# An extra ScalarE copy of a mixed RWKV projection from PSUM to SBUF, one multiply on VectorE, and smaller weight pools in the GLA stage

## The chip, the cores and the metric

The kernel runs on one core of one Trainium2 chip. The metric is the time of one execution on the device in microseconds (us), lower is better. The engines of the core work side by side and each takes its own instructions strictly in the order of its queue: TensorE (PE; its weight loads are listed apart as PEld), VectorE (DVE), ScalarE (ACT), GpSimd (POOL) and SyncE (SP, which here only issues transfers). They wait for each other through semaphores. PSUM is the memory into which TensorE writes its sums; a PSUM bank holds 512 float32 numbers in each of 128 partitions. SBUF is the working memory.

## What is computed

One layer of a decoder: a normalised input `h` (2048 tokens, 1024 channels) is projected once, and the projection feeds three causal mixers (RWKV-7, MLA attention, chunked gated linear attention or GLA), whose gated results are merged and projected again.

```python
h = rms_norm(x, norm_pre); proj = h @ w_in
(c_q, c_kv, k_rope, u_rwkv, g_q, g_k, g_v, g_lat, br_gate, merge_gate) = split(proj)
# RWKV: every channel is mixed with the token before, then split
u_prev = pad(u[:, :-1], one zero row in front)
u = u + (u_prev - u) * mu            # = u * (1 - mu) + u_prev * mu
r, k, v, lw, la = split(u)           # 512, 512, 512, 64, 64 channels
... recurrence over the tokens, head by head ...
y = (y - mean) * rsqrt(var + RWKV_GN_EPS) * ln_w + ln_b + bonus
# merge
ys = stack([y_mla, y_rwkv, y_gla]) * silu(br_gate)
merged = sum(sigmoid(merge_gate) * (ys @ w_branch_out)); x + rms_norm(merged @ w_out)
```

## The kernel before

The program is one stream for each engine, written out by a scheduler: the source is run once, every instruction gets a priority (`tc.high_priority(...)`), and a list scheduler with a modelled timeline sets the order on each engine. So an edit at one place can move instructions at many others. Tiles come from pools with a fixed number of buffers; an instruction that writes a new tile waits until the last reader of the buffer's old tile is done.

The stages follow each other: RWKV (`phase_rwkv`), a short stage for latents, MLA, GLA (`phase_gla`), merge. Matmuls are made in three passes for accuracy: `mm3` (L133 to L135) multiplies the high part of the weights with the high and the low part of `h`, and the low part of the weights with the high part of `h`. Weights therefore go through `load_w` (L121): a transfer issued by SyncE brings `w_raw`, ScalarE rounds it to `w_hi` (L118), and GpSimd subtracts to get `w_lo` (L119). One projection unit takes a block of 512 tokens and 128 output channels: `load_w8` makes four weight parts of 2 x 128 channels each, and each part feeds six matmuls of 128x512, 24 for a unit, all into one PSUM bank. Two banks (`psd0`, `psd1`, both called `psd` in the profile) are used in turn, in the RWKV stage and again in the GLA stage.

In the RWKV stage TensorE is filled with such units. Those of the RWKV input itself go through `mixed` (L387): there are 13 for each of the four blocks of tokens, 52 in all. One of the 13 has a single output tile `lwla` of 512 tokens; the other twelve write `r`, `k` or `v` in two halves of 256 tokens (`outs`, u = 0 and 1), which are separate tiles. `mixed` empties the bank so: for each half ScalarE multiplies by 1 - mu (L395), then VectorE adds mu times the sums shifted by one token (L397). Then VectorE adds the token carried over from the block before (L400) and copies the bank's last column to `carry` (L402). In the built order the ScalarE multiply of the second half waits for the VectorE instruction of the first half: the two engines take turns at the bank. The next unit of this bank starts when L402 is done.

Beside the units run the serial parts of RWKV: `within`, `inverses`, `whole`, `prepare` and `chain` work on 16 groups of 256 tokens and two head pairs. `chain` (L522) ends a group with a normalisation over each head: VectorE computes the inverse root (`k.rsqrt`), GpSimd multiplies `ysb` by it (L590), TensorE turns the result (L594) and VectorE writes `yo` (L600). `plain` and `gates` units fill up TensorE; their banks are emptied by a ScalarE copy (L317).

In the GLA stage the class `Gates` (L884) supplies the filling: 36 gate projections for the first three token blocks. `until` (L910) loads the weights of a gate once (L917, four parts with 4 raw and 5 rounded buffers) and uses them either for one block or for the two blocks 1 and 2 one after the other. There are 108 units of 24 matmuls, 32 of the loads serve two blocks. A ScalarE copy empties each bank (L926) and a transfer writes the result out (L927).

Of the kernel before, what the change touches and what calls it, by code (L numbers as in the profile page):

```python
# [9 lines left out]
F32 = mybir.dt.float32  # L10
# [3 lines left out]
ALU = mybir.AluOpType  # L14
# [10 lines left out]
TB = 512  # L25
# [45 lines left out]
class Ctx:  # L71
# [19 lines left out]
    def pool(self, name, bufs, **kw):  # L91

        if kw.get("space") != DRAM:
            kw["reuse_waits"] = "tile"
        return self.tc.tile_pool(name=name, bufs=bufs, **kw)
# [233 lines left out]
def phase_rwkv(k, pl, x, pos, w_rwkv, w_up2, w_more, w_gate, y_dram, more, pre, rope_dram):  # L329
# [3 lines left out]
    tc, nc = k.tc, k.nc  # L333
    with ExitStack() as st:
# [3 lines left out]
        t1 = pool("rw_t1")  # L338
# [12 lines left out]
        carry = per.tile([128, 13], F32, name="carry")  # L351
# [35 lines left out]
        def mixed(h, n, outs):  # L387


            ps = pl.sums()  # L390
            k.project(ps, pl.weights(w_rwkv[n]), h, slice(0, TB))
            mu = k.p("mu", n)
            m = TB // len(outs)
            for u, o in enumerate(outs):
                nc.scalar.mul(o, ps[:, u * m:u * m + m], imu[:, n:n + 1])  # L395
                i = u == 0
                nc.vector.scalar_tensor_tensor(out=o[:, int(i):m], in0=ps[:, u * m - 1 + i:u * m + m - 1], scalar=mu,  # L397
                                               in1=o[:, int(i):m], op0=ALU.mult, op1=ALU.add)
            o = outs[0]
            nc.vector.scalar_tensor_tensor(out=o[:, 0:1], in0=carry[:, n:n + 1], scalar=mu, in1=o[:, 0:1],  # L400
                                           op0=ALU.mult, op1=ALU.add)
            nc.vector.tensor_copy(carry[:, n:n + 1], ps[:, TB - 1:TB])  # L402

        idx = lambda q, hd, j: q * 4 + j * 2 + hd

# [115 lines left out]

        def chain(G, mr, T, bkt, rv, at):  # L522

            B, g, u, ar, bv, uv = (G[n] for n in ("B", "g", "u", "ar", "bv", "uv"))
            Z = state[g]
            by_head = lambda a: a.rearrange("p (q h v) -> p q h v", q=2, h=2)

# [9 lines left out]
            for cc in range(4):  # L537
                j, e_ = cc // 2, cc % 2
                asl, rsl = halves(e_)
                for q in range(2):  # L540
                    for hd, hs in heads:
                        m = nc.tensor.matmul(pA[:, q, hd], lhsT=ar[hs, q, cc, :], rhs=Z[hs, q, :], start=True, stop=True)
# [5 lines left out]
                for q in range(2):  # L548
                    for hd, osl in enumerate((asl, rsl)):
                        hc = slice((2 * q + hd) * 64, (2 * q + hd) * 64 + 64)  # L550
                        m = nc.tensor.matmul(pU[osl, q * 64:q * 64 + 64], lhsT=T[asl, idx(q, hd, j), :], rhs=rhs[asl, hc],
                                             start=True, stop=True)
# [5 lines left out]
                for q in range(2):  # L558
                    for hd, hs in heads:
                        hc = slice((2 * q + hd) * 64, (2 * q + hd) * 64 + 64)  # L560
                        m = nc.tensor.matmul(pZ[hs, q, :], lhsT=bkt[:, q, cc, hs], rhs=uv[:, j, e_, hc],
                                             start=True, stop=True)
# [18 lines left out]
            y4 = ysb.rearrange("p j (h v) -> p (j h) v", v=64)  # L581
# [5 lines left out]
                nc.scalar.activation(out=ysq, in_=y4[:, 4 * j:4 * j + 4], func=AF.Square)  # L587
                nc.vector.tensor_reduce(out=va[:, 4 * j:4 * j + 4], in_=ysq, axis=AX.X, op=ALU.add)
            rs = k.rsqrt(t2, va, 1.0 / 64, GN_EPS, "gn", bufs=1)
            nc.gpsimd.tensor_tensor(out=y4, in0=y4, in1=rs.unsqueeze(2).broadcast_to([128, 8, 64]), op=ALU.mult)  # L590
            po = ps_q.tile([128, 2, 256], F32, name="psq")
            for q in range(2):
                for j in range(2):
                    m = nc.tensor.transpose(po[:, q, j * 128:(j + 1) * 128], ysb[:, j, q * 128:(q + 1) * 128], k.ident)  # L594
                    if q == j == 0:
                        at(m, 14)
            for q in range(2):
# [3 lines left out]
                                               in1=bv[:, q, :], op0=ALU.mult, op1=ALU.add)  # L601
# [122 lines left out]
        n = 4 * NB  # L724
        blk, G, W, P, R = {}, {}, {}, {}, {}
# [10 lines left out]
        def project_group(i):  # L736
# [3 lines left out]
            if g == 0:  # L740
                lwla = t1.tile([128, TB], F32, name="lwla", bufs=1)
                mixed(blk["h"], 0, [lwla])
                nc.scalar.activation(out=lwla[0:64], in_=lwla[0:64], func=AF.Tanh)
                blk["l"] = lwla
            h, lwla = blk["h"], blk["l"]
            t = {m: [t1.tile([128, 2, 256], F32, name=m, bufs=RB) for _ in range(2)] for m in "rkv"}
            for q in range(2):
                for m in range(3):
                    mixed(h, 1 + 3 * (2 * g + q) + m, [o[:, q, :] for o in t["rkv"[m]]])
# [134 lines left out]
class Gates:  # L884
# [25 lines left out]
    def until(self, share, ps):  # L910

        k, nc = self.k, self.k.nc
        while self.todo and self.done < share * self.units:
            n, blocks = self.todo.pop(0)
            if n == 8 and blocks == (0,) or n == 0 and blocks == (1,):
                self.turned(blocks[0] + 1, ps)
            w = k.load_w8(self.wp, self.w_gate[n], 128, "w", parts=4, rb=4, hb=5)  # L917
            for B in blocks:
                i = self.turn % 2
                self.turn += 1  # L920
                p = self.ps[i].tile([128, TB], F32, name=f"psd{i}")
                k.filling = self.products
                k.project(p, w, self.h[B], slice(0, TB))
                k.filling = None
                o = self.op.tile([128, TB], F32, name="plain", bufs=2)
                nc.scalar.copy(o, p)  # L926
                nc.sync.dma_start(out=self.pre[n][:, B * TB:B * TB + TB], in_=o)  # L927
                self.done += 1
# [634 lines left out]
```

## Time and profile before

| what | value |
|---|---|
| time, three runs | 2982.84 us median (2981.33 to 2990.15) |
| the profiled execution, its own time | 2985.36 us |
| its span in the trace, first instruction to last | 2983.6 us |
| mean granted TensorE clock | 0.982 |
| busy: VectorE, ScalarE, GpSimd | 1718.7 us (58%), 1493.3 us (50%), 1444.3 us (48%) |
| TensorE in the chain that ended last | 65% of the span |

The profile lists busy time for each engine, groups of instructions by source line, and for a group the idle time of its engine just before it with the instruction that ended the wait ("idle before"; the arrow `<-` names who was waited for). Line numbers are those of the kernel before. A matmul row's duration is longer than the distance between two matmuls, since they are pipelined. The granted clock (PEclk) is the share of its full clock that TensorE was given.

### The profile page before, as it was taken

What the parts mean: (1) busy time and instruction counts of PE and PEld (TensorE: products, weight loads), DVE (VectorE), ACT (ScalarE), POOL (GpSimd) and SP (SyncE); (2) the same over time, 40 slices, a digit from 0 to 9 for tenths busy, and PEclk for the clock granted to TensorE, in tenths of its full rate; (3) what the DMA queues carried; (4) which work ended last, traced back from release to release, by engine and by line L of the source; (5) the groups of instructions that cost most, each with busy time, mean ns of one, the idle gap of its engine ahead of it and who ended that gap; (6) DMA issues with size and microseconds to landing.
All of it is one profiled execution on the core that took longest, in us unless ns stands there. A gap on an engine that the chain in (4) does not pass through costs nothing.

```text
span 2983.6 us, 54189 instructions
## 1 busy us (share of the span) xinstructions
PE 2861.1 (96%) x18496; PEld 2309.9 (77%) x18496; DVE 1718.7 (58%) x4642; ACT 1493.3 (50%) x3495; POOL 1444.3 (48%) x1865
## 2 busy tenths in 40 slices
PE   8998999999999999899999999999999999999998
PEld 6676767667777777689999887788788887777887
DVE  4647566666646524488888886544423313875444
ACT  5444444435444436587777775554433334554211
POOL 4543544444445445455454546775444424575322
PEclk9999999999999999899999999999999999999999
DMA  4333333223333434200000024444233226865422
GB/s 134 99 100 103 102 90 111 84 80 91 91 116 84 131 115 142 66 22 18 19 19 16 17 80 141 161 142 130 89 100 102 85 94 221 280 213 192 136 98 78
DMA packets 285173, 312.76 MB, mean 105 GB/s; under 512 B 77904, under 2 KB 234592, under 8 KB 284896
## 3 DMA queue, kind: packets, MB, share of 16 engines
q1 hardware_dynamic: 259088, 278.76, 30.1%
q10 hardware_dynamic: 25808, 30.54, 3.1%
q8 instruction: 146, 2.39, 0.3%
q14 instruction: 131, 1.07, 0.1%
HBM read 233.16 MB, written 76.02 MB: 104 GB/s over the span
## 4 chain that ended last, share of the span: by engine, by line
PE 65%; DVE 9%; DMA 3%; ACT 2%; issue 2%; POOL 1%; SPq 0%; ACTq 0%; DVEq 0%; POOLq 0%
PE psd L133 10%; PE psd L135 10%; PE psd L134 10%; PE pso L1307 4%; PE pst L1285 4%; PE pss L133 3%; PE pss L135 3%; PE pss L134 3%; PE psb L135 2%; PE psg L133 2%; PE psg L135 2%; PE psg L134 2%; PE psb L133 2%; PE psb L134 2%; PE psc L1070 1%
## 5 line engine op out<-in xcount | busy, mean ns | idle before, releaser
L119 POOL TENSOR_TENSOR w_lo<-w_raw,w_hi 128x256 fp32r<-128x256 f32 x848 | 649.9, 774 | 810.8 <-ACT w_hi L118 746.5
L133 PE MATMUL psd<-hh,w_hi 128*128 128x512 f32 x1952 | 798.7, 410 | 16.9 <-DVE carry L402 6.6
L135 PE MATMUL psd<-hh,w_lo 128*128 128x512 f32 x1952 | 787.5, 405 | 9.1 <-POOL w_lo L119 8.7
L134 PE MATMUL psd<-hl,w_hi 128*128 128x512 f32 x1952 | 780.6, 400 | 0.0
L118 ACT CAST w_hi<-w_raw 128x256 fp32r<-128x256 f32 x848 | 337.1, 404 | 532.3 <-PE psd L134 284.0
L133 PEld LDWEIGHTS psd<-hh,w_hi 128*128 128x128 f32 x1952 | 372.4, 191 | 109.1 <-ACT w_hi L118 17.1
L135 PEld LDWEIGHTS psd<-hh,w_lo 128*128 128x128 f32 x1952 | 372.5, 191 | 100.4 <-POOL w_lo L119 18.6
L134 PEld LDWEIGHTS psd<-hl,w_hi 128*128 128x128 f32 x1952 | 372.4, 191 | 75.5 <-issue 3.0
L1270 POOL TENSOR_SCALAR P<-P,nm 128x1024 f32<-128x1024 f32 (+2 forms) x192 | 165.5, 872 | 193.9 <-DVE nm L1267 157.6
L1290 DVE TENSOR_TENSOR tl<-pst,th 128x512 fp32r<-128x512 f32 (+2 forms) x352 | 193.9, 562 | 31.4 <-ACT th L1289 29.8
L1289 ACT CAST th<-pst 128x512 fp32r<-128x512 f32 (+2 forms) x352 | 165.2, 488 | 79.1 <-PE pst L1285 40.5
L1262 ACT ACTIVATE P<-P,nm 128x1024 f32<-128x1024 f32 (+2 forms) x192 | 172.3, 901 | 17.2 <-DVE nm L1258 13.8
L1248 DVE TENSOR_SCALAR_CACHE_REDUCE P<-pss 128x512 f32<-128x512 f32 (+3 forms) x288 | 168.5, 594 | 11.8 <-PE pss L135 8.7
L1285 PE MATMUL pst<-cs,P 128*128 128x128 f32 x1088 | 165.5, 274 | 0.2 <-DVE tl L1290 0.2
L1307 PE MATMUL pso<-th,v 128*128 128x256 f32 x576 | 150.1, 283 | 2.6 <-DVE yo L1315 2.6
L1307 PE MATMUL pso<-tl,v 128*64 128x256 f32 x576 | 139.1, 281 | 0.7 <-DVE tl L1290 0.7
L133 PE MATMUL pss<-kh,qh 128*128 128x512 f32 (+2 forms) x320 | 129.3, 404 | 5.1 <-issue 4.7
L1285 PEld LDWEIGHTS pst<-cs,P 128*128 128x128 f32 x1088 | 125.0, 140 | 8.9 <-DVE tl L1290 0.8
L119 POOL TENSOR_TENSOR wb_lo<-wb_raw,wb_hi 128x256 fp32r<-128x256 f32 x96 | 87.1, 913 | 83.7 <-ACT wb_hi L118 68.6
L1307 PEld LDWEIGHTS pso<-th,v 128*128 128x128 f32 x576 | 108.4, 188 | 12.1 <-DVE yo L1315 2.8
L135 PE MATMUL pss<-kh,ql 128*128 128x512 f32 (+2 forms) x320 | 117.0, 367 | 0.1
L134 PE MATMUL pss<-kl,qh 128*128 128x512 f32 (+2 forms) x320 | 117.0, 366 | 0.0
(391 smaller groups left out, 5640.5 us busy)
## 6 DMA issues: line engine op xcount, KB each, us to landing
w_raw<-in_w_gate_dram SPq DMA_DIRECT2D x448, 128.0 KB, 2.2
pre<-plain SPq DMA_DIRECT2D x144, 256.0 KB, 2.4
w_raw<-in_w_rwkv_dram SPq DMA_DIRECT2D x208, 128.0 KB, 2.2
w_raw<-in_w_more_dram SPq DMA_DIRECT2D x192, 128.0 KB, 2.2
h_g<-pre SPq DMA_DIRECT2D x48, 512.0 KB, 4.9
h_x<-in_x_dram SPq DMA_DIRECT2D x44, 512.0 KB, 4.3
more<-plain SPq DMA_DIRECT2D x48, 256.0 KB, 2.7
wb_raw<-in_w_br_dram ACTq DMA_DIRECT2D x96, 128.0 KB, 3.6
```

What stands on the lines that cost most here:

```text
L118: nc.scalar.copy(hi, src)
L119: (sub or nc.gpsimd).tensor_tensor(out=lo, in0=src, in1=hi.bitcast(F32), op=ALU.subtract)
L133: mm(out, lhsT=lhs[0], rhs=rhs[0], start=start, stop=False)
L134: mm(out, lhsT=lhs[0], rhs=rhs[1], start=False, stop=False)
L135: m = mm(out, lhsT=lhs[1], rhs=rhs[0], start=False, stop=stop)
L1248: nc.vector.tensor_scalar(out=pt[:, c0:c0 + f], in0=s_[:, 0:f], scalar1=-MLA_SCALE, scalar2=3e38, op0=ALU.mult, op1=ALU.min, accum_out=mx[ ...
L1262: nc.scalar.activation(out=pt[:, cw], in_=pt[:, cw], func=AF.Exp, bias=nm[:, 0:1], scale=-1.0, accum_out=nm[:, 1 + n:2 + n])
L1270: nc.gpsimd.tensor_scalar(out=pt[:, cw], in0=pt[:, cw], scalar1=nm[:, 1:2], scalar2=1.0, op0=ALU.mult, op1=ALU.mult)
L1285: nc.tensor.transpose(tp[:, kl, qt, :], P[qt][:, kt * 128:(kt + 1) * 128], k.ident)
L1289: nc.scalar.copy(flat(th)[:, r], flat(tp)[:, r])
L1290: nc.vector.tensor_tensor(out=flat(tl)[:, r], in0=flat(tp)[:, r], in1=flat(th)[:, r].bitcast(F32), op=ALU.subtract)
L1307: nc.tensor.matmul(d_, lhsT=l_, rhs=r_, start=kt == 0 and j == 0, stop=last and kl == 1 and j == 1)
```

## The change

```diff
@@ mixed @@
             for u, o in enumerate(outs):
                 nc.scalar.mul(o, ps[:, u * m:u * m + m], imu[:, n:n + 1])
+
+            now = t1.tile([128, TB], F32, name="now", bufs=2)
+            nc.scalar.copy(now, ps)
+            for u, o in enumerate(outs):
                 i = u == 0
-                nc.vector.scalar_tensor_tensor(out=o[:, int(i):m], in0=ps[:, u * m - 1 + i:u * m + m - 1], scalar=mu,
+                nc.vector.scalar_tensor_tensor(out=o[:, int(i):m], in0=now[:, u * m - 1 + i:u * m + m - 1], scalar=mu,
                                                in1=o[:, int(i):m], op0=ALU.mult, op1=ALU.add)
...
-            nc.vector.tensor_copy(carry[:, n:n + 1], ps[:, TB - 1:TB])
+            nc.vector.tensor_copy(carry[:, n:n + 1], now[:, TB - 1:TB])
@@ chain @@
+            i_ = 4 * B + 2 * g + u
...
-            nc.gpsimd.tensor_tensor(out=y4, in0=y4, in1=rs.unsqueeze(2).broadcast_to([128, 8, 64]), op=ALU.mult)
+            (nc.vector if i_ == n - 1 else nc.gpsimd).tensor_tensor(
+                out=y4, in0=y4, in1=rs.unsqueeze(2).broadcast_to([128, 8, 64]), op=ALU.mult)
@@ Gates.until @@
-            w = k.load_w8(self.wp, self.w_gate[n], 128, "w", parts=4, rb=4, hb=5)
+            w = k.load_w8(self.wp, self.w_gate[n], 128, "w", parts=4, rb=3, hb=3)
```

Three edits. In `mixed` ScalarE reads the bank three times in a row (both multiplies, then a copy of all 512 columns to the SBUF tile `now`), and VectorE takes its shifted operand and the carried column from `now`; the sums stay the same. In `chain` the multiply of the last of the 16 groups goes from GpSimd to VectorE. In `Gates.until` there are 3 raw and 3 rounded weight buffers in place of 4 and 5. In the changed file the lines below `mixed` have other numbers: L395 to L402 become L395, L398 (the copy), L401, L404 and L406; L522 is then the copy L518 of before, L561 and L562 are L556 and L557, and L619 is L613.

ScalarE's queue at the 22nd `mixed` unit (the first `k` of a group), before; `uv` and `ysb` belong to the chain, `sq` to the lengths of `k`, and `ta` to the operands of the next group:

```order
L395 ACTIVATE k<-psd_4406,imu 128x256
L118 CAST w_hi<-w_raw 128x256
L395 ACTIVATE k<-psd_4406,imu 128x256
L613 ACTIVATE sq<-k,pc 128x256
L645 ACTIVATE ta<-psm,half 128x256 x4
```

The same unit in the changed kernel:

```order
L395 ACTIVATE k<-psd_4448,imu 128x256 x2
L398 COPY now<-psd_4448 128x512
L522 COPY rv<-psq 128x512
L561 COPY uv_1845<-psc 64x2x64 x2
L562 COPY ysb<-psc 64x256
L619 ACTIVATE sq<-k,pc 128x256
```

The two multiplies and the copy now stand together. Of the 48 ScalarE multiplies that waited for VectorE before, 2 do now, and 10 of the 52 copies wait for VectorE to be done with an older `now`.

VectorE's queue at the same unit, before, and then in the changed kernel:

```order
L397 SCALAR_TENSOR_TENSOR k<-psd_4406,pc,k 128x255
L400 SCALAR_TENSOR_TENSOR k<-carry,pc,k 128x1
L397 SCALAR_TENSOR_TENSOR k<-psd_4406,pc,k 128x256
L402 COPY carry<-psd_4406 128x1
L451 TENSOR_TENSOR xtmp<-xm,xt 128x62
```

```order
L404 SCALAR_TENSOR_TENSOR k<-carry,pc,k 128x1
L401 SCALAR_TENSOR_TENSOR k<-now,pc,k 128x255
L401 SCALAR_TENSOR_TENSOR k<-now,pc,k 128x256
L406 COPY carry<-now 128x1
L427 TENSOR_TENSOR ma_3887<-psm,cs 128x256
```

The number of VectorE instructions is the same; none of the four reads the bank any more, and they stand in one run.

TensorE in the late GLA stage, at the boundary between the two blocks that share one gate's weights (the two units are `psd_28441` and `psd_28469`, `hh` and `hl` are the high and low part of `h`), before:

```order
L133 MATMUL psd_28441<-hh_23231,w_hi 128x512
L134 MATMUL psd_28441<-hl_23232,w_hi 128x512
L135 MATMUL psd_28441<-hh_23231,w_lo 128x512
L133 MATMUL psd_28469<-hh_25579,w_hi 128x512
L134 MATMUL psd_28469<-hl_25580,w_hi 128x512
L135 MATMUL psd_28469<-hh_25579,w_lo 128x512
```

The end of the same pair of units in the changed kernel, where they are `psd_28545` and `psd_28573`:

```order
L135 MATMUL psd_28573<-hh_25693,w_lo 128x512
L133 MATMUL psd_28545<-hh_23333,w_hi 128x512
L134 MATMUL psd_28545<-hl_23334,w_hi 128x512
L133 MATMUL psd_28573<-hh_25695,w_hi 128x512
L134 MATMUL psd_28573<-hl_25696,w_hi 128x512
L135 MATMUL psd_28545<-hh_23333,w_lo 128x512
L133 MATMUL psd_28545<-hh_23335,w_hi 128x512
L134 MATMUL psd_28545<-hl_23336,w_hi 128x512
L135 MATMUL psd_28545<-hh_23335,w_lo 128x512
L135 MATMUL psd_28573<-hh_25695,w_lo 128x512
L133 MATMUL psd_28573<-hh_25697,w_hi 128x512
L134 MATMUL psd_28573<-hl_25698,w_hi 128x512
```

Before, the first unit was finished, all 24 matmuls, ahead of the second. With three buffers the fourth weight part has a buffer only when the first part has served both blocks, so three parts run for the first block, three for the second, and the fourth part for both at the end; the first bank is finished only four matmuls before the second. Apart from these places the order of the RWKV stage, of the end of MLA, of GLA and of the start of the merge has shifted in many small ways, while most of MLA is untouched.

More of the change, by code (lines that the diff above doesn't have):

```diff
@@ L522, in chain @@
         def chain(G, mr, T, bkt, rv, at):
-            B, g, u, ar, bv, uv = (G[n] for n in ("B", "g", "u", "ar", "bv", "uv"))
+            B, g, u, ar, bv, uv = (G[n_] for n_ in ("B", "g", "u", "ar", "bv", "uv"))
+            i_ = 4 * B + 2 * g + u
             Z = state[g]
```

## The prediction

> **What bounds the kernel now.** I read the page first, then busy time in stretches cut at the stage boundaries, then, for the stages that the edits touch, the groups of each engine with the idle time before them.
>
> ```profile
> PE 2861.1 (96%) x18496; PEld 2309.9 (77%) x18496; DVE 1718.7 (58%) x4642; ACT 1493.3 (50%) x3495; POOL 1444.3 (48%) x1865
> ...
> 20.00:930.00 910.00, 854.42 (x6089) 647.34 (x6088) 557.00 (x1505) 416.81 (x1018) 429.15 (x558) 0.96 0.34 98
> 930.00:1220.00 290.00, 286.67 (x2067) 219.32 (x2065) 119.35 (x315) 148.45 (x392) 144.68 (x210) 0.99 0.41 124
> 1220.00:1260.00 40.00, 27.51 (x169) 22.20 (x170) 18.32 (x68) 15.20 (x40) 13.88 (x17) 0.74 0.10 30
> 1760.00:2010.00 250.00, 235.92 (x1586) 192.85 (x1585) 152.54 (x309) 138.54 (x350) 171.64 (x265) 0.99 0.47 150
> 2010.00:2480.00 470.00, 467.93 (x3074) 380.77 (x3073) 154.85 (x360) 182.65 (x455) 204.54 (x324) 1.00 0.32 102
> ```
>
> The stretches list length, then busy time of PE, PEld, DVE, ACT and POOL, then the granted clock. TensorE is the bound everywhere, so an edit counts only by the TensorE gaps that it closes or opens, and by the clock that follows a gap. In the part of the RWKV stage that holds all 52 mixed units (20 to 930 us) there are 910 - 854.4 = 55.6 us of gaps, and the clock is 0.96. The later GLA stretch has 2.1 us of gaps in 470: nothing can be won there, only lost.
>
> ```profile
> L133 PE MATMUL psd<-hh,w_hi 128*128 128x512 f32 x803 | 336.1, 421 | 13.4 <-DVE carry L402 6.6 <-ACT w_hi L118 5.5 <-ACT sq L613 1.3
> L135 PE MATMUL psd<-hh,w_lo 128*128 128x512 f32 x803 | 330.9, 415 | 7.1 <-POOL w_lo L119 6.8
> L561 PE MATMUL psc<-uv,bkt 128*64 128x64 f32 x360 | 20.9, 236 | 2.5 <-ACT ysb L557 2.4
> ...
> L395 ACT ACTIVATE r<-psd,imu 128x256 f32<-128x256 f32 x32 | 15.1, 472 | 13.3 <-DVE r L397 13.3
> L395 ACT ACTIVATE v<-psd,imu 128x256 f32<-128x256 f32 x32 | 15.1, 472 | 26.0 <-DVE v L397 25.9
> L395 ACT ACTIVATE k<-psd,imu 128x256 f32<-128x256 f32 x32 | 15.1, 471 | 10.3 <-DVE k L397 10.1
> ```
>
> These are groups of the same stage. TensorE waited 6.6 us for the bank (`carry`), 12.3 us for weights, and a little for other ScalarE work. ScalarE itself stood 49.3 us (13.3 + 25.9 + 10.1) inside the emptying of banks, waiting for VectorE, with weight casts and chain copies queued behind. The largest case, ScalarE, then VectorE, then TensorE, and the clock around it:
>
> ```profile
> 596.95 0.47 ACT L395 ACTIVATE r<-psd,imu 128x256 f32<-128x256 f32 x1
> 602.26 0.47 ACT L395 ACTIVATE r<-psd,imu 128x256 f32<-128x256 f32 x1 [4.30 <-DVE r L397]
> ...
> 600.78 1.06 DVE L167 SCALAR_TENSOR_TENSOR gn_y<-gn_t,gn_y 128x8 f32<-128x8 f32 x1
> 601.76 0.47 DVE L397 SCALAR_TENSOR_TENSOR r<-psd,pc,r 128x255 f32<-128x255 f32 x1
> 603.24 0.14 DVE L402 COPY carry<-psd 128x1 f32<-128x1 f32 x1
> ...
> 603.53 0.77 PE L133 MATMUL psd<-hh,w_hi 128*128 128x512 f32 x1 [3.41 <-DVE carry L402]
> ...
> 597.00:603.00 6.00, 3.12 (x20) 1.97 (x18) 5.86 (x14) 1.56 (x5) 4.48 (x5) 1.00 0.38 91
> 603.00:610.00 7.00, 5.86 (x25) 4.18 (x26) 2.14 (x5) 1.32 (x5) 3.74 (x5) 0.52 0.27 73
> 531.00:535.00 4.00, 4.00 (x16) 3.03 (x12) 4.00 (x14) 1.55 (x4) 3.17 (x4) 0.57 0.10 33
> 924.00:928.00 4.00, 4.00 (x18) 2.78 (x17) 3.06 (x12) 1.26 (x3) 2.42 (x3) 0.57 0.47 82
> ...
> 529.24 0.47 ACT L395 ACTIVATE v<-psd,imu 128x256 f32<-128x256 f32 x1 [3.08 <-DVE v L397]
> 920.33 0.47 ACT L395 ACTIVATE k<-psd,imu 128x256 f32<-128x256 f32 x1 [1.29 <-DVE k L397]
> ```
>
> The second multiply came 5.3 us after the first, because VectorE reached its own first half late; the bank came free at 603.4, TensorE had stood 3.41 us, and the next 7 us ran at a granted clock of 0.52. The two last rows are stalls of the same kind, each just ahead of another of the dips above.
>
> **Edit 1, what it removes.** In the changed order nothing stands between ScalarE and the bank but ScalarE: two multiplies of 0.47 and a copy of 512 columns, about 1.5 us, against 5.4 us that the other bank's 24 matmuls give. What hangs on the turn-taking: the bank waits, 6.6 us; the wait for `sq`, 1.3, and nearly all of that for `ysb`, 2.4, which ScalarE makes next after the stalls at 920 and 529. That is 10.3 us. The clock dips behind three of these gaps cost at most 7 x 0.48 + 4 x 0.43 + 4 x 0.43 = 6.8 us. Together 17.1 us, and more only where weights came late behind a stall; least 0, if other work is late at the same places. I take **-13**, since the order around every one of these places has moved and ScalarE's queue stays strict.
>
> **Edit 1, what it adds.** 52 copies on ScalarE. The same shape:
>
> ```profile
> L317 ACT COPY plain<-psd 128x512 f32<-128x512 f32 x83 | 48.4, 583 | 9.1 <-DMA more<-plain 8.1 <-PE psd L135 0.2
> ...
> L706 DVE SCALAR_TENSOR_TENSOR r<-r,pc,ld x32: 471/832/1498, 62.9 to 967.4; 128x256 f32<-128x256 f32 x32
> L397 DVE SCALAR_TENSOR_TENSOR k<-psd,pc,k x32: 465/480/485, 42.9 to 922.5; 128x255 f32<-128x255 f32 x16, 128x256 f32<-128x256 f32 x16
> ```
>
> 52 x 0.583 = 30.3 us of ScalarE, less than the 49.3 us of standing that goes, so the copies lie in time that was lost; where that cover is missing, chain copies and casts come 0.58 us later. VectorE's shifted additions now have both tensors in SBUF, as L706 has (least, median, largest ns): its median is 832 against 480 with one in PSUM, and its spread is wide. That bounds the 96 half-width additions between 0 and 96 x 0.35 = 34 us more of VectorE, on 557 of 910. In return VectorE no longer stands at L397 for ScalarE's second half. TensorE's waits on VectorE's chain work would grow with its load, by some 6%; I take **+2**, between -2 and +10.
>
> **Edit 2.** The last group of the chain, on GpSimd and then TensorE, with VectorE's instruction of the size that takes its place:
>
> ```profile
> 1233.29 0.69 DVE L584 TENSOR_TENSOR ysb<-ysb,mu__13689 128x512 f32<-128x512 f32 x1
> 1237.83 0.17 DVE L167 SCALAR_TENSOR_TENSOR gn_y<-gn_t,gn_y 128x8 f32<-128x8 f32 x1
> ...
> 1238.14 1.04 POOL L590 TENSOR_TENSOR ysb<-ysb,gn_y 128x512 f32<-128x512 f32 x1 [16.44 <-DVE gn_y L167]
> ...
> 1239.24 1.12 PE L594 MATMUL psq<-cs,ysb 128*128 128x128 f32 x4 [7.39 <-POOL ysb L590]
> ```
>
> TensorE waits for nothing else there. 0.69 in place of 1.04, and 0.1 of the handover, make **-0.5**; the 7 us of VectorE work ahead stay.
>
> **Edit 3.** In GLA the last of three buffers must be enough to cover the cast and the subtraction. The trace has no GLA with three buffers, but the RWKV stage loads all its weights with three. The weight casts of the two RWKV stretches and of GLA, and TensorE's weight waits in the quiet RWKV stretch and in GLA:
>
> ```profile
> 20.00:930.00 910.00, 159.51 (x401) 0.96 0.34 98
> 930.00:1220.00 290.00, 68.53 (x190) 0.99 0.41 124
> 1760.00:2010.00 250.00, 49.65 (x126) 0.99 0.47 150
> 2010.00:2480.00 470.00, 65.03 (x163) 1.00 0.32 102
> ...
> L133 PE MATMUL psd<-hh,w_hi 128*128 128x512 f32 x285 | 116.9, 410 | 0.7 <-ACT w_hi L118 0.7
> L135 PE MATMUL psd<-hh,w_lo 128*128 128x512 f32 x285 | 116.7, 409 | 1.1 <-POOL w_lo L119 1.0
> ...
> L135 PE MATMUL psd<-hh,w_lo 128*128 128x512 f32 x806 | 317.5, 395 | 0.9 <-POOL w_lo L119 0.9
> ```
>
> Three buffers cost 12.3 / 401 = 31 ns per part with the chain at work and 1.7 / 190 = 9 ns without. For the 289 casts of GLA that is 2.6 to 8.9 us against 0.9 now, so +1.7 to +8.0; I take **+5**. There is a second price. Where two blocks share a gate, the first bank now ends four matmuls before the second, and the next unit wants it at once; the order has 22 places with four matmuls and at most four small ones in between. Four matmuls are issued in
>
> ```profile
> 2000.41 0.39 PE L133 MATMUL psd<-hh,w_hi 128*128 128x512 f32 x1
> 2001.32 0.39 PE L134 MATMUL psd<-hl,w_hi 128*128 128x512 f32 x1
> ```
>
> 0.91 us, and the bank's copy takes 0.58 after the last matmul's own tail of 0.16: hidden, by 0.17 less the handovers, if ScalarE is free. It is busy 39% of the time there (182.65 of 470). At 0.1 us each I take **+2**, between 0 and one more instruction of 0.6 us in front at each place, 13.
>
> **The sum.** -13 + 2 - 0.5 + 5 + 2 = -4.5 us. The profiled execution took 2985.36 us (span 2983.6 and 1.8 around it), so 2980.9; it lay 2.5 us above the median of the three runs, so against that median **2978 us**. About 0.3% or 9 us is what a measurement of this kernel can tell from no change; the forecast is inside it.
>
> **Rivals.** *More is freed than I can trace.* A ScalarE that never stands still inside a bank may bring casts and chain copies early everywhere, also where I put a gap down to VectorE or a transfer. The stretch loses 55.6 us to gaps and 910 x 0.04 = 36 us to the clock; if a third of these 92 goes, with 7 us lost in GLA, the time is about 2960. For it: the dips at 531 and 924 followed stalls shorter than the one at 603, so small shifts pay twice. Against: nothing in the chain's own work or its transfers gets shorter.
>
> *GLA starves where gates share weights (the slower side).* For each of 32 shared loads the fourth part is loaded only after the second block has begun, its cast and subtraction standing behind GLA's own ScalarE and GpSimd work. The cover is 12 matmuls, 2.7 us, with GpSimd 69% busy (171.64 of 250). If a shared load loses 0.9 us on top of my sum, 32 x 0.9 = 29 us, the time is 3007; the change is a measurable loss from 0.45 us per load on (14 us). Against: RWKV's units live with the same 2.7 us.
>
> *VectorE and GpSimd block each other.* If every new addition takes L706's time and holds up GpSimd's subtractions as much, the 34 us spread over both engines; with a third of that on TensorE, 11 us, Edit 1 is worth only 2 and the time is about 2987, no measurable change. The row at 600.78 shows the mechanism: an operation on 8 columns took 1.06 us there and 0.17 at 1237.83. The Trainium skill, page "SBUF — State Buffer", section "Who interferes with whom", says that a VectorE instruction with two SBUF inputs contends with a GpSimd instruction that reads SBUF, for one shared port, and with one SBUF input does not; by that rule this change moves 100 additions to the bad side. The trace agrees: L397's 480 ns never spread beyond 485, L706's reached 1498.
>
> *The turn-taking remains.* If ScalarE waits for VectorE elsewhere, at the 12 multiplies and copies that still wait for old tiles, Edit 1 gives nothing and GLA's 7 us remain: about 2990.
>
> **How the numbers follow.** Forecast 0.44, more freed 0.22, starving 0.17, blocking 0.12, turn-taking 0.05. The order moved at hundreds of places, and one spell like that at 603 more or less is 3.41 + 3.4, some 7 us either way: a quarter of the forecast is faster than 2974, an eighth slower than 2992. So faster 0.22 + 0.11 = 0.33; slower 0.17 x 0.9 + 0.05 and 0.04 from the last two rivals, 0.24; same 0.43. The range: low end, all 17.1 us, one spell less, 2 from VectorE, Edit 2 and only 1.7 lost in GLA, 2982.8 - 17.1 - 7 - 2 - 0.5 + 1.7 = 2958; high end, no gain in RWKV and 16 lost in GLA, 8.0 for weights and 8 of the 13 for banks, 2999.
>
> **What would show it.** Right: waits of L395 for VectorE under 5 us in all, no TensorE wait on `carry`, fewer half-clock spells before 930 us, PE gaps there down by 8 to 15 us; VectorE's additions at 480 to 830 ns; weight and bank waits in GLA at 4 to 15 us. The last wait for `ysb` near 6.9 us. Wrong: RWKV gaps unchanged or dozens lower, GLA gaps over 20 us, or a difference in MLA or the merge, where I count none.

## The result, and the profile after

The changed kernel takes **3041.40 us** (median of 6 runs, 3035.40 to 3047.26) against 2983.94 for the kernel before on the same chip: ratio 1.0185, 95% interval [1.0173, 1.0197]. It is slower by 1.85%, some 55 us by the ratio, and outside the range of the prediction. The profiled execution took 3035.4 us; its mean granted clock is 0.984 against 0.982, so the clock does not explain the loss.

The same stretches as in the prediction, from the kernel after (length, busy time of PE, PEld, DVE, ACT and POOL, granted clock):

```profile
20.00:930.00 910.00, 854.69 (x6084) 647.55 (x6083) 567.88 (x1480) 440.76 (x1072) 432.30 (x558) 0.97 0.34 97
930.00:1220.00 290.00, 284.36 (x2064) 217.33 (x2064) 123.47 (x338) 146.59 (x388) 143.77 (x210) 0.99 0.42 126
1760.00:2010.00 250.00, 233.59 (x1502) 177.24 (x1500) 146.32 (x299) 129.25 (x320) 158.50 (x246) 0.99 0.42 137
2010.00:2480.00 470.00, 454.68 (x2929) 354.08 (x2928) 151.38 (x355) 177.69 (x445) 201.32 (x320) 1.00 0.30 96
```

RWKV as a whole is as it was: 55.3 us of TensorE gaps where there were 55.6, and 6084 matmuls where there were 6089. The last matmul of the stage starts 2 us later than before, MLA's last one at the same time (1761 us). The late GLA stretch went from 2.1 to 15.3 us of gaps and does 145 matmuls less in its 470 us. But 15 us of gaps are not 55: the rest is inside what the profile calls busy. It shows when the gate matmuls alone (those into `psd`) are counted in equal stretches. First the kernel before, then after:

```profile
1960.00:2060.00 100.00, 87.19 (x360) 66.86 (x360) 0.00 (x0) 8.67 (x15) 1.00 0.44 138
2160.00:2260.00 100.00, 88.10 (x373) 69.19 (x372) 0.00 (x0) 9.32 (x16) 1.00 0.31 101
2260.00:2360.00 100.00, 85.64 (x361) 66.80 (x360) 0.00 (x0) 8.76 (x15) 1.00 0.27 89
```

```profile
1960.00:2060.00 100.00, 80.13 (x306) 54.58 (x304) 0.00 (x0) 7.57 (x13) 1.00 0.37 117
2160.00:2260.00 100.00, 82.31 (x328) 60.91 (x327) 0.00 (x0) 8.17 (x14) 0.98 0.28 90
2260.00:2360.00 100.00, 81.06 (x330) 60.27 (x329) 0.00 (x0) 8.18 (x14) 1.00 0.29 96
```

The counts in brackets behind the second number are matmuls into the gate banks. They fall by 9 to 15%, the PE busy time only by 5 to 8%. A gate matmul is listed for 0.389 us in the median of both kernels, while the next one usually starts 0.227 us after it, so a delay of up to 0.16 us lies inside the listed time of the matmul ahead; some of the delayed ones are listed as longer too (42 of 304 took more than 0.4 us from 1960 to 2060 us, 17 of 360 before). Taken from the starts of neighbouring gate matmuls in the two traces, the usual distance is 0.227 us; distances over 0.3 us were 114 before with 17.7 us above the usual, and are 252 with 51.7 now, so +34. From its first to its last gate matmul the stage lost 51 us; the other 17 lie where one of two neighbours, or both, are other matmuls. Changes between gate matmuls and others went from 223 to 365.

The idle times before TensorE's weight loads (PEld) say what was waited for. The columns are total us, number and longest; "issue" stands where the engine waited for nothing that the profile shows, and L1070 (L1076 after) makes GLA's score matmuls. GLA before, then after:

```profile
PEld psc L1070 <- issue: 17.0, 78, 0.4
...
PEld psd L133 <- ACT plain L926: 2.0, 2, 1.2
...
PEld psd L135 <- POOL w_lo L119: 1.3, 1, 1.3
```

```profile
PEld psc L1076 <- issue: 36.0, 127, 0.6
PEld psd L135 <- POOL w_lo L119: 15.1, 23, 2.8
PEld psd L133 <- ACT plain L932: 14.4, 14, 3.2
PEld psd L133 <- ACT w_hi L118: 10.7, 20, 2.1
```

3.3 us of waits for weights and banks (its largest rows of that kind) have become 40.2, in 57 waits of 0.7 us on average. The score matmuls' row rose by 19.0 us besides; of its waits, 12 followed a gate's weight load before and 73 do now, so this part goes with the changes between gate and score matmuls. Together the rows rose by 56 us, against 51 lost in GLA; weight loads overlap matmuls, so they need not agree to the microsecond. By both counts about two thirds of the loss are waits for weights and banks, and a third lies at the changes. One of the long waits, in the timeline after (start, duration, engine, line; in brackets the idle time before and who ended it):

```profile
1855.78 0.41 ACT L118 CAST w_hi<-w_raw 128x256 fp32r<-128x256 f32 x1
1856.09 0.41 ACT L118 CAST w_hi<-w_raw 128x256 fp32r<-128x256 f32 x1
...
1856.87 0.57 POOL L1050 TENSOR_TENSOR e<-b 128x128 f32<-128x128 f32 x1 [0.29 <-DVE qk L1053]
1858.00 0.40 PE L134 MATMUL psd<-hl,w_hi 128*128 128x512 f32 x1
1858.04 0.46 POOL L1050 TENSOR_TENSOR e<-b 128x128 f32<-128x128 f32 x1 [0.59 <-DVE qk L1053]
1859.08 0.90 POOL L1050 TENSOR_TENSOR e<-b 128x128 f32<-128x128 f32 x1 [0.59 <-DVE qk L1053]
1859.94 1.56 POOL L119 TENSOR_TENSOR w_lo<-w_raw,w_hi 128x256 fp32r<-128x256 f32 x2
1860.72 0.50 PE L135 MATMUL psd<-hh,w_lo 128*128 128x512 f32 x1 [2.32 <-POOL w_lo L119]
```

Both casts are done at 1856.5. GpSimd could subtract at once, but in its queue three of GLA's own subtractions (L1050) stand ahead, each waiting for VectorE's `qk`, so `w_lo` starts 3.4 us later and TensorE stands 2.32 us.

### The profile page after: what moved, and what is told of

It reads as the page before. It is cut to its first block, busy times and chain, and to the rows that moved or that the text cites. A ratio compares the mean times of both kernels' runs of the same rounds, so it can differ in the third digit from the quotient of the medians.

```text
span 3033.6 us, 54165 instructions
## 1 busy us (share of the span) xinstructions
PE 2892.6 (95%) x18496; PEld 2305.7 (76%) x18496; DVE 1729.8 (57%) x4643; ACT 1519.9 (50%) x3547; POOL 1448.0 (48%) x1864
## 4 chain that ended last, share of the span: by engine, by line
PE 64%; DVE 9%; DMA 5%; issue 2%; POOL 2%; ACT 2%; SPq 0%; ACTq 0%; POOLq 0%; DVEq 0%
PE psd L133 10%; PE psd L135 10%; PE psd L134 9%; PE pso L1313 4%; PE pst L1291 4%; PE pss L133 3%; PE pss L135 3%; PE pss L134 3%; PE psc L1076 2%; PE psb L135 2%; PE psg L135 2%; PE psg L133 2%; PE psg L134 2%; PE psb L133 2%; PE psb L134 2%
## 5 line engine op out<-in xcount | busy, mean ns | idle before, releaser
L119 POOL TENSOR_TENSOR w_lo<-w_raw,w_hi 128x256 fp32r<-128x256 f32 x848 | 652.4, 776 | 842.6 <-ACT w_hi L118 766.1
L133 PE MATMUL psd<-hh,w_hi 128*128 128x512 f32 x1952 | 809.8, 416 | 20.7 <-ACT plain L932 9.9
L133 PEld LDWEIGHTS psd<-hh,w_hi 128*128 128x128 f32 x1952 | 372.7, 191 | 120.2 <-ACT w_hi L118 21.9
L133 PE MATMUL pss<-kh,qh 128*128 128x512 f32 (+2 forms) x320 | 129.3, 404 | 3.3 <-POOL kh L1218 2.9
L119 POOL TENSOR_TENSOR wb_lo<-wb_raw,wb_hi 128x256 fp32r<-128x256 f32 x96 | 88.7, 930 | 85.3 <-ACT wb_hi L118 63.7
L1089 DVE TENSOR_TENSOR bm<-psc,cs 128x384 f32<-128x384 f32 x32 | 17.8, 556 | 182.3 <-PE psc L1076 181.0
```

Source lines behind the costliest of these rows:

```text
L119: (sub or nc.gpsimd).tensor_tensor(out=lo, in0=src, in1=hi.bitcast(F32), op=ALU.subtract)
L133: mm(out, lhsT=lhs[0], rhs=rhs[0], start=start, stop=False)
```

## Experiments

Theory: with only three rounded buffers in the gates TensorE catches up with casts and subtractions whose queues are now and then held up. Rivals: the changed order of the program, the copy in `mixed`, or the weights shared by two blocks. Every ratio below is against the kernel before on the same chip. Line numbers of an edit are left out; "before" and "after" name the kernel that is edited.

**The changed kernel with the old weight pools.**

```diff
-            w = k.load_w8(self.wp, self.w_gate[n], 128, "w", parts=4, rb=3, hb=3)
+            w = k.load_w8(self.wp, self.w_gate[n], 128, "w", parts=4, rb=4, hb=5)
```

> The changed kernel with 4 raw and 5 rounded weight buffers in GLA again; the copy to SBUF and the last multiply on VectorE stay. Theory 1 (all of the loss is the smaller weight pools): time 2970 to 2985, GLA from the end of MLA to the last gate matmul 755 to 765 us as before (758 there, 809 in the changed kernel). Theory 2 (the copy's re-ordering of the whole program also slows GLA): 2995 to 3030, GLA 775 to 800 us. The RWKV stage ends at 1242 us under both, so the copy is worth 0 +- 8 us.

2981.57 us, ratio 0.9991 [0.9980, 1.0002]. The whole loss is gone: it is Edit 3, and the first two edits together are no change that can be told from none.

**The small pools alone**, in the kernel before, with both counts lowered, the raw blocks alone, and the rounded ones alone:

```diff
-            w = k.load_w8(self.wp, self.w_gate[n], 128, "w", parts=4, rb=4, hb=5)
+            w = k.load_w8(self.wp, self.w_gate[n], 128, "w", parts=4, rb=3, hb=3)   # both
+            w = k.load_w8(self.wp, self.w_gate[n], 128, "w", parts=4, rb=3, hb=5)   # raw
+            w = k.load_w8(self.wp, self.w_gate[n], 128, "w", parts=4, rb=4, hb=3)   # rounded
```

> The kernel before with only the weight pools of GLA cut to 3 raw and 3 rounded buffers. Theory 1: 3030 to 3040, with the whole loss in GLA (about 50 us). Theory 2: 2990 to 3015.

> The kernel before with 3 raw buffers and still 5 rounded ones in GLA. If the transfers of raw weights come too late (their landing of 2.2 us, then cast and subtraction, in a ring of three), most of the loss is here: 3015 to 3035. If the rounded buffers are what is short, 2980 to 2992.

> The kernel before with 4 raw and only 3 rounded buffers in GLA. If the rounded buffers are what is short: 3020 to 3040. If the raw ones are: 2980 to 2995. If either is enough to starve TensorE, this and the run with 3 raw buffers both lose 20 us or more.

Both: 3035.03 us, 1.0169 [1.0150, 1.0187]. Raw: 2993.73, 1.0027 [1.0017, 1.0038]. Rounded: 3040.39, 1.0186 [1.0169, 1.0204]. The rounded buffers alone give all of it; the raw ones cost 8 us alone and nothing on top.

**How it depends on the depth**: four rounded buffers, and six with five raw blocks.

```diff
+            w = k.load_w8(self.wp, self.w_gate[n], 128, "w", parts=4, rb=4, hb=4)
+            w = k.load_w8(self.wp, self.w_gate[n], 128, "w", parts=4, rb=5, hb=6)
```

> The kernel before with four rounded buffers in the gates instead of five (raw blocks stay at four). Theory depth (every buffer fewer shortens the lead of the casts over the matmuls): the loss of two buffers, 55 us, comes in steps, so about 3000 to 3015 us. Theory four parts (a gate's weights are four parts, and only below four must a cast wait inside the unit that it belongs to): within 0.3% of before, 2976 to 2994 us. Theory order (the program's order of TensorE changes with the buffers, and each additional switch between gate matmuls and score matmuls costs about 0.1 us): this one has 30 and 28 switches against 18 and 12 before, so about 3 us, 2984 to 2990.

> The kernel before with one raw block and one rounded buffer more in the gates (five and six). Theory depth with a knee at five: no change, 2978 to 2988 us. Rival (five still bind: ScalarE's casts wait 116 us for TensorE's matmuls in the GLA stage of before): 10 to 25 us faster, 2958 to 2974.

Four: 2997.23 us, 1.0042 [1.0019, 1.0065]. Six: 2978.63, 0.9981 [0.9969, 0.9992]. So 6, 5, 4, 3 buffers stand at -6, 0, +12 and +55 us: no step at the four parts of a gate, and not even steps either; each buffer less costs two to four times the one before. The rival of the second run, 10 to 25 us from ScalarE's idle time, fell: with six buffers the wait of the casts for a buffer is still there,

```profile
ACT w_hi L118 <- PE psd L134: 138.0, 160, 4.8
```

and only 6 us came of it. This wait is 116.4 us with five buffers and 163.1 with three in the changed kernel, where 55 us are lost, so its size does not tell whether the pool is deep enough. What counts is TensorE's own wait; with four buffers

```profile
PEld psd L135 <- POOL w_lo L119: 4.9, 11, 0.8
PEld psd L133 <- ACT w_hi L118: 4.6, 8, 1.1
PEld psd L133 <- ACT plain L926: 0.3, 1, 0.3
```

9.8 us, against 3.3 and 40.2 above; the score matmuls' row is 21.2 there.

**Which half of the weights.** Pools of different depth for `w_hi` and `w_lo`:

```diff
-        hi = pool.tile(shape, F32R, name=tag + "_hi", bufs=hb)
-        lo = pool.tile(shape, F32R, name=tag + "_lo", bufs=hb)
+        hi = pool.tile(shape, F32R, name=tag + "_hi", bufs=hh or hb)   # 5, then 3
+        lo = pool.tile(shape, F32R, name=tag + "_lo", bufs=hl or hb)   # 3, then 5
```

> The kernel before with five buffers for the high halves and three for the low halves of the gates' weights. Theory high halves (ScalarE's cast waits until the second matmul with the part three back, and what stands behind it in ScalarE's queue waits too): the loss is gone, 2980 to 2995 us. Theory low halves (GpSimd's subtraction stands late in its queue, and the last matmul of each part waits for it): the loss stays, 3025 to 3045. Theory order: 57 and 59 switches against 12 and 18 before, and 75 in the kernel that has three of both; at some 0.1 to 0.2 us each 9 to 17 us, 2993 to 3003.

> The kernel before with three buffers for the high halves and five for the low halves of the gates' weights; TensorE's order is that of the kernel with three of both but for a few rows. Theory high halves: the loss stays, 3030 to 3042 us. Theory low halves: the loss goes, 2980 to 2995. Theory order: the loss stays, as far as it comes from the order.

Three for `w_lo` alone: 3021.88 us, 1.0136 [1.0116, 1.0156], which no theory had. Three for `w_hi` alone: 3037.16, 1.0180 [1.0165, 1.0196]. By the ratios these are 41 and 54 us, and both together make 55: they don't add. That the shorter of the two pools sets how far the weights can be ahead fits this, but not why three for `w_lo` cost 13 us less; no run shows that.

**A faster subtraction with three buffers.**

```diff
+            w = k.load_w8(self.wp, self.w_gate[n], 128, "w", parts=4, rb=4, hb=3, sub=nc.vector)
```

> The kernel before with three rounded buffers in the gates, and their subtractions on VectorE instead of GpSimd. Theory lead (a part's refill, cast and subtraction, must end inside the two parts of matmuls that three buffers give, 2.7 us; on GpSimd it misses that where other work stands ahead of it, and on VectorE the subtraction of some 0.4 us instead of 0.76 has a shorter queue ahead): 15 to 40 us of the 55 come back, 3000 to 3025 us. Theory order (TensorE's order as with three buffers, 74 switches each way between gate and score matmuls): the loss stays, 3033 to 3045. Rival (VectorE gets the stage's serial work late in exchange): 3040 or more.

3021.74 us, 1.0125 [1.0111, 1.0140]: 18 us less than with GpSimd (1.0186), though TensorE's order has as many changes between gate and score matmuls as there, and their row is 36.0 us as in the changed kernel. The subtraction takes 0.47 us in the mean here, 0.76 on GpSimd before, and it stands in another queue. The time of a refill counts, by the one or the other; with a third of the loss back it is not all.

**Order or waits.** Five buffers, but in the written order each cast and subtraction stands behind the matmuls on the part three back, as if there were three. The dependency only orders the program; the chip waits for nothing more.

```diff
+            while self.tied < min(len(self.parts), len(self.reads) + 3):
+                for a, b in zip(self.parts[self.tied], self.reads[self.tied - 3]):
+                    k.tc.add_manual_dep(a, b.name, mybir.DependencyInfo(
+                        mybir.DependencyClass.NoSync, mybir.DependencyReason.DATA), reason="place")
+                self.tied += 1
```

> The kernel before, five rounded buffers, but each cast and subtraction of the gates is tied in the written order behind the matmuls on the part three back (an order only, no wait on the chip). Theory waits (three buffers cost because the chip waits for a buffer): within 0.3% of before, 2977 to 2993 us. Theory order (three buffers cost because casts are written later into ScalarE's and GpSimd's queues, behind other work): a large part of the 55 us, 3005 to 3040.

2983.30 us, 0.9992 [0.9983, 1.0002]. In its GLA stage (lines shifted) the waits of the weight loads are

```profile
PEld psd L136 <- ACT plain L935: 0.9, 2, 0.7
PEld psd L138 <- POOL w_lo L120: 0.5, 2, 0.3
```

1.4 us. ScalarE's casts wait 59 us for a buffer there, against 116 in the kernel before, so they are indeed written later; it costs nothing as long as there are buffers. TensorE's own order in this kernel is not that of three buffers, so that was tried from the other side: three buffers, and the score matmuls tied together.

```diff
+                        ga.behind(e_, ga.done - AHEAD + p)   # for each of these 20 score matmuls
+                ga.ahead(e_, ga.done - AHEAD + p)
...
+    def ahead(self, m, units):
+        at = int(units * NC8)
+        if 0 <= at < len(self.products):
+            self.k.tc.add_manual_dep(self.first[at], m.ins.name, mybir.DependencyInfo(
+                mybir.DependencyClass.NoSync, mybir.DependencyReason.DATA), reason="place")
```

> Three rounded buffers as in the kernel with the whole loss, with the score matmuls tied together in TensorE's order: 48 switches from gate to score matmuls and 51 back, against 76 and 75 (12 and 18 in the kernel before). Theory waits: the loss stays, 3033 to 3045 us. Theory order (the switches): some 50 of the 120 additional ones go, at 0.1 us each, or more where the order is all of it: 5 us to half of the loss less, 3010 to 3033.

3032.54 us, 1.0156 [1.0138, 1.0174]. That is between the two ranges, some 9 us below the kernel with three rounded buffers (1.0186 [1.0169, 1.0204]), with intervals that overlap. If the loss went with the number of changes between gate and score matmuls, of which less than half of the additional ones are taken away, some 31 us would be left; 47 are. So these changes are not most of it. 9 us for 43% of the additional changes make some 21 for all of them, with a wide interval, near the 17 and 19 us that the trace of the changed kernel has at them; the score matmuls' row (lines shifted) fell to

```profile
PEld psc L1083 <- issue: 25.9, 96, 0.4
```

against 37.1 with three rounded buffers, while the waits of the same kind ahead of gate matmuls rose from 2.4 us to 6.7. That the changes cost a third of the loss is thus read from traces and agrees with this run, but no run takes them away alone.

**Shared weights.** Each gate's weights loaded for one block at a time, with three and with five buffers:

```diff
-        self.todo += [(i, (1, 2)) for i in range(self.LAG, n)] ...
+        self.todo += [(i, (B,)) for i in range(self.LAG, n) for B in (1, 2)] ...
...
+            w = k.load_w8(self.wp, self.w_gate[n], 128, "w", parts=4, rb=4, hb=3)   # in the run with three
```

> Three rounded buffers, and every gate's weights loaded for one token block at a time: 108 loads instead of 76, none shared. Theory sharing (the prediction's rival: buffers are short where two units hold one gate's parts): the loss goes, within 10 us of the same kernel with five buffers. Theory lead (three buffers give two parts of lead, whose length is 2.7 us of matmuls for a single unit and twice that for a shared pair): the loss grows, 50 to 90 us above the same kernel with five buffers.

> The same 108 unshared loads with five rounded buffers, to set the last run against. 128 casts (0.405 us each, 52 us of ScalarE), 128 subtractions (0.76 us, 98 us of GpSimd) and their loads come in addition, on engines that are half busy there: 2985 to 3010 us under either theory.

Three: 3067.36 us, 1.0268 [1.0248, 1.0288]. Five: 2992.36, 1.0023 [1.0010, 1.0036]. Without sharing three buffers cost 73 us instead of 55 (by the ratios), so sharing is not what starves TensorE. Per load the loss is about the same, 55 / 76 = 0.72 us and 73 / 108 = 0.68, so this run cannot tell the shorter time that a part lasts from the greater number of refills. With three buffers and no sharing the waits are

```profile
PEld psd L135 <- POOL w_lo L119: 22.5, 40, 2.3
PEld psd L133 <- ACT w_hi L118: 19.6, 35, 2.3
PEld psd L133 <- ACT plain L926: 1.2, 6, 0.2
```

More for weights, and nearly all of the waits for a bank, 14.4 us in the changed kernel, are gone: those do belong to the shared pairs. The score matmuls' row is 54.9 us here and 16.8 with five buffers.

**The bytes of three buffers in six of half the size.**

```diff
+            w = k.load_w8(self.wp, self.w_gate[n], 128, "w", parts=8, rb=8, hb=6)
```

> The gates' weights in eight parts of half the size, with six rounded buffers: the SBUF of three buffers of the whole size. Theory lead (what counts is the time that the buffers ahead hold, against the time of a refill): five halves ahead are five times 0.68 us, 3.4 us, between the 2.7 us of three buffers (3037) and the 4.1 us of four (2997), so 3000 to 3030 us. Rival (twice as many casts and subtractions, each with its fixed time, lengthen the queues by as much): 3035 or more.

3028.72 us, 1.0159 [1.0124, 1.0194]. The median lies in the theory's range, but the interval takes in the kernel with three buffers (1.0186): inconclusive.

**The first two edits, each alone** in the kernel before, **and both with deeper pools** in the kernel after:

```diff
+            now = t1.tile([128, TB], F32, name="now", bufs=2)       # first run, with `now` read as in the change
+            nc.scalar.copy(now, ps)
...
-            nc.gpsimd.tensor_tensor(out=y4, ...)                    # second run
+            (nc.vector if 4 * B + 2 * g + u == n - 1 else nc.gpsimd).tensor_tensor(out=y4, ...)
...
-            w = k.load_w8(self.wp, self.w_gate[n], 128, "w", parts=4, rb=3, hb=3)   # third run
+            w = k.load_w8(self.wp, self.w_gate[n], 128, "w", parts=4, rb=5, hb=6)
```

> The kernel before with the copy to `now` alone. Theory of the prediction (the copy takes 13 us of waits away and adds 2): about 2974 us. Theory moved wait (the waits for `carry` go, and as long waits on the chain of the inverse come in their place, as the profile of the changed kernel has them; both edits together measured no change): within 0.2% of before, 2979 to 2990 us. Rival (two edits that cancel): 6 us or more on one side, and the other edit alone as much on the other.

> The kernel before with the last group-norm product alone moved from GpSimd to VectorE. All theories: it is used once, on the path between RWKV's last output and the next stage, 1044 ns to 691 ns, so -0.4 us, not to be told from none: 2980 to 2989 us. Rival (two edits that cancel): several us slower or faster.

> The changed kernel with five raw blocks and six rounded buffers in the gates. Theory independent parts: the ratio of the first two edits, 0.9991, times that of the deeper pools on the kernel before, 0.9981, gives 0.9972 of before, 2977 us (2972 to 2983). Rival (the gain of the deeper pools was noise or the same as the edits' gain): 2980 to 2987.

The copy alone: 2980.93 us, 0.9988 [0.9977, 0.9998]. The last multiply alone: 2988.06, 1.0009 [0.9997, 1.0021]. Both with five raw and six rounded buffers: 2981.11, 0.9994 [0.9984, 1.0005]. No two edits that cancel, and the small gains of the parts don't add up. No version is better than the kernel before by more than 0.2% in the ratio.

## Why the prediction was wrong

**Edit 3, weights: this step failed.** It took +5 us (+1.7 to +8.0) from "three buffers cost 12.3 / 401 = 31 ns per part with the chain at work and 1.7 / 190 = 9 ns without". In the changed kernel GLA's weight loads wait 25.8 us for `w_hi` and `w_lo`, 24.5 more than before, and the whole edit costs 50 to 55 us. The price was read from the wrong view: the 12.3 us are idle times of TensorE's *matmuls*. In the same stretch, 20 to 930 us of the kernel before, the weight *loads* waited

```profile
PEld psd L133 <- ACT w_hi L118: 15.2, 16, 3.8
PEld psd L135 <- POOL w_lo L119: 14.6, 22, 4.5
```

29.8 us for the same operands, 74 ns per part; GLA's 304 casts (the prediction counted the 289 up to 2480 us) at that price are 22 us, near the 24.5. So the view explains most of this term. The Trainium skill, page "Perfetto Trace Analysis", section "Identifying the Most-Contended Engine", says that matmul busy time misjudges how near TensorE is to its limit and points to the busy time of the weight loads; the stretch of GLA from 1960 to 2060 us above agrees, where gate matmuls fell by 15%, their weight-load time by 18% (66.86 to 54.58) and their matmul time by 8%.

That a rate from RWKV fits GLA is luck as far as is known, since the stages have other work. The account that the runs support is one of time: how long a refill takes in GLA, against how long the parts ahead keep TensorE going, and both could be read from the trace of before. A part feeds six matmuls, 6 x 0.227 = 1.36 us, so five buffers hold 5.4 us ahead (four parts), four hold 4.1, three 2.7. From the last matmul on a buffer's old part to the end of the new subtraction the 299 refills of the kernel before took some 1.6 us in the median (in the mean the cast is 0.405 of it and the subtraction 0.763), but 3.5 at the upper quartile, 5.4 at nine tenths and 7.2 at 95%. Longer than 5.4, 4.1 and 2.7 us were about 30, 57 and 100 of them. These counts rise as the losses do (0, +12, +55), but they give neither their size nor the zero: not every slow refill was needed at once, and a shared part lasts twice as long. A quicker subtraction takes 18 us back, and a late order without a short pool costs nothing, which fits.

**Edit 3, banks.** Taken at +2, bounded by 13. The waits of L133 for `plain` rose by 12.4 us (2.0 to 14.4): the mechanism was right, the size was that of the bound.

**Edit 3, changes between matmuls.** The sum had no term for them, though GLA's order was known to have shifted. By the two counts of the trace they hold 17 to 19 us. So +5, +2 and 0 stood where the rows show 24.5, 12.4 and 19.

**The rival "GLA starves where gates share weights"** had the sign and the stage, and at 3007 less than half of the loss. Its place was wrong: by the ends of the 108 gate units in the two traces, 33 of the 51 us that GLA lost were lost by the 40th unit, the last ahead of the shared pairs, and without any sharing the loss is larger. The banks' 12.4 us are what sharing does cost. Its argument against itself, that RWKV's units "live with the same 2.7 us", fell with the view: they live with the 30 us of waits above.

**Edit 1, what it removes (-13).** The signs at the bank came, those in TensorE did not. No TensorE wait for `carry` is left, and ScalarE's three reads of the bank follow each other:

```profile
L398 ACT COPY now<-psd 128x512 f32<-128x512 f32 x52 | 30.3, 586 | 0.0
L395 ACT ACTIVATE r<-psd,imu 128x256 f32<-128x256 f32 x32 | 13.9, 475 | 3.9 <-PE ps L715 3.8
L395 ACT ACTIVATE v<-psd,imu 128x256 f32<-128x256 f32 x32 | 13.5, 470 | 0.1
L395 ACT ACTIVATE k<-psd,imu 128x256 f32<-128x256 f32 x32 | 13.4, 468 | 1.5 <-PE psd L135 1.4
```

49.3 us of waits for VectorE are gone. But the gaps did not fall by 8 to 15 us (gaps unchanged were named as a sign of being wrong), the spells near half the clock before 930 us are 11 in both traces (64.9 and 61.4 us), and the time did not follow: the edit alone is worth 3.6 us (0.12%, interval 0.02 to 0.23%). Of TensorE's longest waits in the stretch these were there before, and these are now:

```profile
PE psq L477 <- DVE xt L473: 7.5, 6, 2.6
PE psd L135 <- POOL w_lo L119: 6.8, 8, 4.0
PE psd L133 <- DVE carry L402: 6.6, 6, 3.4
...
PE psc L542 <- DVE z L529: 5.2, 4, 2.2
PE psc L551 <- DVE rhs L546: 3.5, 4, 1.3
```

```profile
PE psd L135 <- POOL w_lo L119: 10.8, 13, 4.3
PE psc L547 <- DVE z L534: 8.3, 4, 3.5
PE psc L556 <- DVE rhs L551: 6.3, 4, 1.9
```

6.6 us for `carry` went, and 4.0, 3.1 and 2.8 came at `w_lo`, `z` and `rhs`; with shifts both ways at others, such as 4.2 less at `xt`, the gaps are 55.3 us in all, as before. The prediction had this as the lower bound, "if other work is late at the same places". Of the forecast -13 + 2 a third is left. That the new waits come from the same late VectorE work is likely from where they stand, and was not tested by itself.

**Edit 1, what it adds (+2).** VectorE's half-width additions have the median of before, 480 ns, and some of them are longer:

```profile
L401 DVE SCALAR_TENSOR_TENSOR r<-now,pc,r x32: 468/480/1340, 35.4 to 913.2; 128x255 f32<-128x255 f32 x16, 128x256 f32<-128x256 f32 x16
```

(least, median, greatest). The largest before was 485. Of all 96, 22 took more than 0.5 us, and each of these 22 overlapped a GpSimd instruction by at least 0.3 us, most often the subtraction of L119; before, 64 of the 96 overlapped one by more than 0.1 us and none took longer than 0.485. (Of the other 74 now, 23 overlapped one by more than 0.1 us too and took no longer.) The rule of the Trainium skill, page "SBUF — State Buffer", section "Who interferes with whom", agrees with that spread. Over all 96 the busy time grew by 10 us, not by the 34 that the median of L706 allowed. So the traces bear out the rival of blocking engines in kind, at a third of its size on VectorE; what that cost in time no run shows.

**Edit 2 (-0.5).** The multiply took 0.69 us as forecast, but the wait was to fall to 6.9 us and did not:

```profile
1240.57 0.69 DVE L595 TENSOR_TENSOR ysb<-ysb,gn_y 128x512 f32<-128x512 f32 x1
...
1241.32 1.11 PE L600 MATMUL psq<-cs,ysb 128*128 128x128 f32 x4 [8.22 <-DVE ysb L595]
```

The VectorE work ahead of it is what TensorE waits for. The edit alone measured 1.0009 [0.9997, 1.0021], no change that can be told, as the forecast had it.

**The range.** Its high end, 2999, took 16 us for the worst of GLA from the two prices for weights and banks, so the same wrong view set the middle and the end. The stage had been named as the one where "nothing can be won, only lost"; a bound from the length of refills against the cover would have opened the range on that side.

## What to carry to other kernels

Before a pool of prepared operands is made smaller, set the slow tail of its refill (from the last use of a buffer to the next operand being ready) against the time of work that the remaining buffers hold, in the stage at hand: here the median of 1.6 us fitted into every cover and the loss still grew steeply, from 12 to 55 us with one buffer less. Look at the changes of order that the smaller pool brings as well. Price TensorE's waits from the weight-load rows and from the number of matmuls in equal stretches, since short delays stand inside its busy time. How long a producer waits for a free buffer does not tell what more buffers would bring; after a stall is removed, look for what was late behind it before the stall is booked as a gain.

## What the runs showed of the hardware

- Short delays hide in TensorE's busy time, since a gate matmul is listed for 0.389 us and the next starts after 0.227: per gate matmul, PE busy time went from 87.19 / 360 = 0.242 us to 80.13 / 306 = 0.262 in the stretch from 1960 to 2060 us.
- The stall of 2.32 us that ended at 1860.72 was followed by a low clock, 0.55 from 1861.5 to 1865 us, where matmuls start 0.43 us apart instead of 0.23:

```profile
1861.50:1865.00 3.50, 3.50 (x13) 2.75 (x11) 3.42 (x10) 2.54 (x6) 1.03 (x3) 0.55 0.29 96
```

- GLA of the changed kernel has three such spells of 3.4 us, each behind an idle time of TensorE of 2.3 to 3.2 us; another idle time of 2.45 us had none, nor had those up to 1.7 us. GLA of the kernel before has one. Two more spells of 3.4 us at about half the clock are some 3 us by estimate, so the clock adds little to the 55 us.
- VectorE additions of 128x256 from PSUM and SBUF took at most 0.485 us; with both tensors in SBUF 22 of 96 took 0.59 to 1.34 us, all of them beside a GpSimd instruction.
